# A two-layer decoder trunk on one core: first weights over two queues, joint roots for two projections

## The chip, the cores and the metric

The kernel runs on one core of a Trainium2 chip. A core has five engines that work through their own instruction queues and wait for each other by semaphores: TensorE (PE, matrix products, with its weight loads shown apart as PEld), VectorE (DVE), ScalarE (ACT), GpSimd (POOL) and SyncE (SP), which here does nothing but issue transfers. Transfers from the chip's memory run on 16 DMA engines and can be issued from several engines' queues. The metric is the time of one execution on the device in microseconds (us), smaller is better; the kernel before takes 554.64 us, the median of three runs.

## The reference

The reference is a decoder trunk of two layers over 256 tokens of width 1024, in float32. Layer 0 uses multi-head latent attention, layer 1 a block attention that, at this length, is plain causal attention with a relative bias. Both are followed by a squared-ReLU MLP.

```python
h = rms_norm(x, attn_norm[0])
proj = h @ w_in                                   # 1024 -> 384 (c_q) + 256 (c_kv) + 64 (k_pe)
q  = rms_norm(c_q, q_a_norm) @ w_uq               # 8 heads of 128 + 64
kv = rms_norm(c_kv, kv_a_norm) @ w_ukv            # 8 heads of 128 + 128
q_nope, q_pe = rms_norm(q[..., :128]), rope(rms_norm(q[..., 128:]))
k_nope, v, k_pe = rms_norm(kv[..., :128]), kv[..., 128:], rope(rms_norm(k_pe))
x = x + mla_attention(q_nope, q_pe, k_nope, k_pe, v) @ w_o
x = x + relu(rms_norm(x) @ w_in_mlp) ** 2 @ w_out_mlp
# layer 1: the same frame with moba_mixer in place of mla_mixer
```

The change touches the first product `proj`, the norms of the keys and queries of the first four heads (`k0`, `q0`), and the loading of the tables of the relative bias.

## The kernel before

**Precision and tiling.** Every large product is made of three: a float32 factor is split into a high part, rounded to the fast float32 format, and a low part, the rest, and high*high, high*low and low*high are added up in PSUM. For each piece of weights (a *unit*, up to 128 x 1024) ScalarE casts the high part (`hi`, line 176) and VectorE subtracts it for the low part (`lo`, line 185). Units are numbered in the order of use: 0 to 7 hold the rows of `w_in`, each with the matching 256 columns of the transposed input, then come nine units of the up-projections (`w_u`), the output projection and so on. `load_one` (line 151) issues the transfer of a unit on SP's queue, `load_raw` keeps a few ahead.

**Order.** The schedule is written out by hand: each engine runs its instructions in the order in which the program emits them. A call in the program is thus a place in the queue of each engine that it uses.

**First product (lines 437 to 530).** For each of the eight row blocks `make_h` (line 271) multiplies the input by the norm's gain on ScalarE (`hTh`, line 274) and makes the low part on VectorE (`hTl`, line 275). Unit 0 is cast in two column groups, the 320 key and value columns by VectorE (line 443) and the 384 query columns by ScalarE (line 445). `lat_mm` (line 459) multiplies. For unit 0 it takes the key columns of both token halves before the query columns, for the others both column groups of one token half after the other. Unit 0 also carries 42 columns of gains. The position table `rowp` is issued after unit 3 (line 233). After the sixth row block the key latent is finished, copied by ScalarE (line 515) and VectorE (line 517) and transposed by TensorE (line 505). Before that copy, ScalarE squares the token-wise input (line 472) and casts the first unit of `w_u`.

**Second stage (lines 800 to 890).** `proj0(name, t)` multiplies one projection for one token half `t`. The names are `k0`, `p` (the rotary part of the queries), `q0`, `v0`, and later `k1`, `v1`, `q1`. `post0` squares it on ScalarE, sums the squares per head (`Norm`, lines 327 to 337; with `on_act` ScalarE does the sums) and calls `root_by` (line 350): an addition of the scaled EPS on VectorE (line 353) and a power of -1/2 on GpSimd (`rsqrt_into`, line 264). `rows0` (`rows_by`, line 356) multiplies by the root on VectorE (line 358), `turn0` transposes on TensorE (line 366) and copies on ScalarE. There is one root for each name and token half. `mean_squares` (line 816) makes for each of the three latents the mean square (line 817) and its product with EPS (line 818). Beside this GpSimd turns the rotary key: two scalings (line 839), a product (line 840), two sums (line 851), and VectorE does it for the queries (`rope_rows`, lines 791 and 792; `rope_sum`, line 798). In the queue of GpSimd the scalings and the product stand ahead of the roots of `p`, the sums ahead of the roots of `q0`.

**Tables.** `table_loads` (line 253) loads the positions, spread to all partitions, and a table of key positions and bias steps in two transfers, in the first MLP.

## Time and profile before

| what | us |
|---|---|
| time, median of three runs (554.51 to 554.75) | 554.64 |
| time of the profiled execution | 554.76 |
| its span, from first to last instruction | 552.8 |
| TensorE busy | 547.9 |
| VectorE busy | 393.3 |
| ScalarE busy | 304.4 |
| GpSimd busy | 93.9 |

The span is what the trace covers; the rest of the profiled execution's time lies around it. Shares of busy time are taken over the whole span. A stage with a limit of its own, such as the first 45 us here, is read from the timeline, where each row has its start, its length, the engine, the line of the program, the operation, what it writes and reads, and in brackets how long the engine stood idle before it and for whom.

### The profile page before, as it was taken

How to read it: one execution, taken by the hardware profiler on the slowest of the kernel's cores; microseconds unless marked ns; L12 is line 12 of the kernel's file. 1: busy time of each engine (PE TensorE's matmuls, PEld its weight loads, DVE VectorE, ACT ScalarE, POOL GpSimd, SP SyncE). 2: the span in 40 equal slices, each digit the busy share in tenths (PEclk: the TensorE clock that was granted, in tenths of full speed). 3: DMA queues.
4: the chain of work that ended last, by engine and by line, in shares of the span. 5: the costliest groups of instructions: out<-in, count | busy, mean ns of one | idle time of the engine just before them, and what ended most of it. 6: DMA issues, size and time to landing. Idle time of an engine off the chain costs nothing.

```text
span 552.8 us, 11397 instructions
## 1 busy us (share of the span) xinstructions
PE 547.9 (99%) x4649; PEld 538.0 (97%) x4649; DVE 393.3 (71%) x651; ACT 304.4 (55%) x497; POOL 93.9 (17%) x109
## 2 busy tenths in 40 slices
PE   8999999999999999999999999999999999999997
PEld 7988999999999999999999999999999999999997
DVE  6897877688997689866677366766867653977630
ACT  7998675665433365445365466746755332656420
POOL 6882100031222000012232100000130311000100
PEclk9999999999999999999999999999999999999999
DMA  8854535686566466555565454345865764665810
GB/s 340 294 173 131 174 112 159 190 277 189 192 197 194 125 217 200 181 171 172 160 221 176 168 154 152 115 153 154 253 218 176 240 194 139 194 213 166 277 39 28
DMA packets 28035, 100.64 MB, mean 182 GB/s; under 512 B 3184, under 2 KB 3696, under 8 KB 27856
## 3 DMA queue, kind: packets, MB, share of 16 engines
q1 hardware_dynamic: 27648, 99.01, 55.6%
q0 software_dynamic: 336, 0.92, 0.4%
q8 instruction: 36, 0.59, 0.4%
q14 instruction: 15, 0.12, 0.1%
HBM read 98.87 MB, written 1.05 MB: 181 GB/s over the span
## 4 chain that ended last, share of the span: by engine, by line
PE 98%; DMA 1%; ACT 0%; DVE 0%; issue 0%
PE ps L85 96%; PE ps L366 2%; PE ps L588 1%; DMA xw<-in_xw 1%; PE ps L505 0%; ACT hTh L274 0%; DVE t L1062 0%; PE ps L878 0%
## 5 line engine op out<-in xcount | busy, mean ns | idle before, releaser
L185 DVE TENSOR_TENSOR wl<-raw,wh 128x1024 fp32r<-128x1024 f32 x177 | 218.5, 1252 | 35.9 <-ACT wh L176 35.3
L176 ACT CAST wh<-raw 128x1024 fp32r<-128x1024 f32 x177 | 182.7, 1047 | 69.5 <-PE ps L85 52.2
L85 PE MATMUL ps<-a,wh 128*128 128x256 f32 x1024 | 175.0, 276 | 0.0
L85 PEld LDWEIGHTS ps<-a,wh 128*128 128x128 f32 x1024 | 154.8, 188 | 0.0
L85 PE MATMUL ps<-hTl,wh 128*128 128x256 f32 x512 | 141.7, 277 | 0.0
L85 PE MATMUL ps<-a,wl 128*128 128x256 f32 x512 | 141.7, 277 | 0.0
L85 PE MATMUL ps<-hTh,wl 128*128 128x256 f32 x512 | 141.4, 276 | 0.0
L85 PE MATMUL ps<-hTh,wh 128*128 128x256 f32 x512 | 141.3, 276 | 0.0
L85 PEld LDWEIGHTS ps<-hTl,wh 128*128 128x128 f32 x512 | 96.1, 188 | 0.1
L85 PEld LDWEIGHTS ps<-hTh,wh 128*128 128x128 f32 x512 | 96.1, 188 | 0.1
L85 PEld LDWEIGHTS ps<-a,wl 128*128 128x128 f32 x512 | 96.1, 188 | 0.0
L85 PEld LDWEIGHTS ps<-hTh,wl 128*128 128x128 f32 x512 | 96.1, 188 | 0.0
L929 ACT ACTIVATE t<-ps 128x512 f32<-128x512 f32 (+1 forms) x34 | 19.4, 572 | 62.4 <-PE ps L85 62.3
L85 PE MATMUL ps<-aT,wh 128*128 128x256 f32 (+1 forms) x256 | 50.2, 288 | 0.0
L931 DVE SCALAR_TENSOR_TENSOR t<-ps,t 128x512 f32<-128x512 f32 (+1 forms) x34 | 22.4, 659 | 36.1 <-ACT t L929 35.9
L85 PE MATMUL ps<-wh,hTh 128*128 128x256 f32 (+2 forms) x224 | 45.5, 289 | 0.8 <-ACT hTh L274 0.8
L85 PE MATMUL ps<-wh,hTl 128*128 128x256 f32 (+2 forms) x224 | 44.6, 283 | 0.0
L85 PE MATMUL ps<-wl,hTh 128*128 128x256 f32 (+2 forms) x224 | 44.3, 283 | 0.0
L85 PEld LDWEIGHTS ps<-aT,wh 128*128 128x128 f32 x256 | 40.3, 188 | 0.2
L85 PE MATMUL ps<-aT,wl 128*128 128x256 f32 x128 | 35.6, 278 | 0.0
L601 ACT ACTIVATE hTh<-x,gains 128x256 fp32r<-128x256 f32 x24 | 12.2, 510 | 42.2 <-POOL x L1053 25.8
L85 PEld LDWEIGHTS ps<-wh,hTh 128*128 128x128 f32 x224 | 34.3, 188 | 1.1 <-ACT hTh L274 1.0
(167 smaller groups left out, 645.5 us busy)
## 6 DMA issues: line engine op xcount, KB each, us to landing
raw<-in_w_in_mlp SPq DMA_DIRECT2D x64, 512.0 KB, 4.3
raw<-in_w_out_mlp SPq DMA_DIRECT2D x64, 512.0 KB, 4.3
raw<-in_w_qkv SPq DMA_DIRECT2D x24, 512.0 KB, 4.4
raw<-in_w_u SPq DMA_DIRECT2D x8, 512.0 KB, 6.7
xw<-in_xw SPq DMA_DIRECT2D x7, 480.0 KB, 6.3
raw<-in_w_o0a SPq DMA_DIRECT2D x4, 512.0 KB, 3.5
raw<-in_w_o0b SPq DMA_DIRECT2D x4, 512.0 KB, 3.6
raw<-in_w_o1a SPq DMA_DIRECT2D x4, 512.0 KB, 4.2
```

The lines of the kernel that those rows point to most:

```text
L85: nc.tensor.matmul(o, a, b, start=start, stop=stop)
L176: (eng.copy if eng is nc.scalar else eng.tensor_copy)(his[i][:, :w], raws[i][:, :w])
L185: eng.tensor_sub(los[i][:, :w], raws[i][:, :w], f32(his[i][:, :w]))
L366: nc.tensor.transpose(pt[:, i * P:(i + 1) * P], yf[:, i * P:(i + 1) * P], ident)
L588: nc.tensor.transpose(pt[:, i * P:(i + 1) * P], self.p[:, i * P:(i + 1) * P], ident)
L601: nc.scalar.activation(hTh[:, k], x[:, k], AF.Copy, scale=gain(gname, k))
L929: nc.scalar.activation(rl, src, AF.Relu)
L931: nc.vector.scalar_tensor_tensor(sq, src, 0.0, rl, op0=OP.max, op1=OP.mult)
```

## The change

- Unit 0 comes in two transfers on SP's queue: first the 320 key and value columns with the input and the gains, then the 384 query columns. Weights now stand ahead of the input in a unit. Unit 1 is issued on ScalarE's queue instead of SP's, and `rowp` follows after unit 1 instead of unit 3.
- For row block 0 ScalarE makes `hTh` for the first 128 tokens and VectorE for the others. Unit 1 is cast in the two column groups, and its products take the key columns of both token halves first, like those of unit 0.
- `k0` and `q0` have one root for both token halves: the sums of squares go side by side into one tile, and after the second half one VectorE instruction adds EPS and one GpSimd power makes both roots. `p`, `k1` and `q1` keep a root for each half.
- The product with EPS of the rotary key's mean square, which nothing reads, is left out.
- In the second stage the projection and the root of `p`'s first half are emitted ahead of the rotary key's scalings and product; `k0`'s second rows go behind the `hi` and `lo` that followed them; `q0`'s second half goes ahead of the `lo` and of `p`'s second rows. `hi` keeps its place among ScalarE's instructions.
- The rings of the small norm tiles have 16 divided by their width buffers instead of 4.
- The positions stand in the table, and one transfer loads both.

```diff
@@ -153,9 +153,10 @@
             raw = early.tile([P, S + n + (0 if i else NG)], F32, name=f"xw{i}")
-            nc.sync.dma_start(raw, src)
-            x0.append(raw[:, :S])
-            raws.append(raw[:, S:S + n])
+            for c in (slice(QR, S + n + NG), slice(0, QR)) if i == 0 else (slice(0, S + n),):
+                (nc.scalar if i == 1 else nc.sync).dma_start(raw[:, c], src[:, c])
+            raws.append(raw[:, :n])
+            x0.append(raw[:, n:S + n])
             if i == 0:
@@ -229,14 +230,14 @@
         load_one()
-        if k == 3:
+        if k == 1:
             nc.sync.dma_start(rowp, A["rowp"])
...
     load_raw()
-    pos_row = const.tile([P, S], I32)
-    tables = const.tile([P, S // 4 + 8 * H], I32)
-    pos_k4, tcur, tprev = (tables[:, :S // 4], *(f32(tables[:, S // 4 + i * 4 * H:S // 4 + (i + 1) * 4 * H]) for i in range(2)))
+    tables = const.tile([P, S + S // 4 + 8 * H], I32)
+    pos_row, pos_k4 = tables[:, :S], tables[:, S:S + S // 4]
+    tcur, tprev = (f32(tables[:, S + S // 4 + i * 4 * H:S + S // 4 + (i + 1) * 4 * H]) for i in range(2))
     ident = const.tile([P, P], F32)
@@ -251,7 +252,6 @@
     def table_loads():
-        nc.sync.dma_start(pos_row, A["pos_row"].to_broadcast([P, S]))
         nc.sync.dma_start(tables, A["tables"])
@@ -271,7 +271,10 @@
         g = gain(gname, k) if k else gains0[0][:, GOFF[gname][0]:GOFF[gname][0] + 1]
-        nc.scalar.activation(hTh[:, k], x0[k], AF.Copy, scale=g)
+        n = S if k else P
+        nc.scalar.activation(hTh[:, k, :n], x0[k][:, :n], AF.Copy, scale=g)
+        if n < S:
+            nc.vector.tensor_scalar(hTh[:, k, n:], x0[k][:, n:], g, None, op0=OP.mult)
         nc.vector.scalar_tensor_tensor(hTl[:, k], x0[k], g, f32(hTh[:, k]), op0=OP.mult, op1=OP.subtract)
@@ -324,10 +327,10 @@
-        def __init__(self, p, width, on_act=False):
+        def __init__(self, p, width, on_act=False, ss=None):
             self.p, self.width, self.nh = p, width, 512 // width
             j = t2(512)
-            self.ss = small.tile([P, self.nh], F32, name="hss", tag=f"hss{self.nh}")
+            self.ss = small.tile([P, self.nh], F32, name="hss", tag=f"hss{self.nh}", bufs=16 // self.nh) if ss is None else ss
             if on_act:
@@ -337,7 +340,7 @@
         def root(self, sq):
-            self.rs = small.tile([P, self.nh], F32, name="hrs", tag=f"hrs{self.nh}")
+            self.rs = small.tile([P, self.nh], F32, name="hrs", tag=f"hrs{self.nh}", bufs=16 // self.nh)
             nc.vector.tensor_scalar(self.ss, self.ss, sq, EPS, op0=OP.mult, op1=OP.add)
@@ -349,7 +352,7 @@
-            self.rs = small.tile([P, self.nh], F32, name="hrs", tag=f"hrs{self.nh}")
+            self.rs = small.tile([P, self.nh], F32, name="hrs", tag=f"hrs{self.nh}", bufs=16 // self.nh)
             nc.vector.tensor_scalar(self.ss, self.ss, 1.0 / self.width, e, op0=OP.mult, op1=OP.add)
@@ -437,7 +440,13 @@
     for k in range(KD):
-        if k == 0:
+        if k == 1:
+            his.append(wsp.tile([P, 1024], F32R, name="wh", tag="wh"))
+            make_h(k, "attn0")
+            for c in win_parts:
+                nc.scalar.copy(his[1][:, c], raws[1][:, c])
+            lo()
+        elif k == 0:
             his.append(wsp.tile([P, 1024], F32R, name="wh", tag="wh"))
@@ -472,7 +481,7 @@
     for k in range(KD - 2):
-        if k == 0:
+        if k < 2:
             for i in range(3):
@@ -764,17 +773,29 @@
-    def post0(name, t, root=True, on_act=False):
+    pairs = {}
+
+    def post0(name, t, on_act=False):
         p = open_p.pop((name, t))
...
             nc.scalar.activation(flat(hd[int(name[1])]["v"][:, t]), p, AF.Copy, scale=scl[:, 0, t:t + 1])
-        else:
-            norms[name, t] = Norm(p, PE_D if name == "p" else P, on_act)
-            if root:
-                root0(name, t)
-
-    def root0(name, t):
-        norms[name, t].root_by(epsm[:, 0 if name[0] == "k" else 2, t:t + 1])
+            return
+        width = PE_D if name == "p" else P
+        if name in ("p", "k1", "q1"):
+            norms[name, t] = Norm(p, width, on_act)
+            norms[name, t].root_by(epsm[:, 0 if name[0] == "k" else 1, t:t + 1])
+            return
+        if t == 0:
+            pairs[name] = small.tile([P, NT, 512 // width], F32, name="pss_" + name, bufs=1)
+        norms[name, t] = Norm(p, width, on_act, pairs[name][:, t])
+        if t == NT - 1:
+            ss, n = pairs[name], 512 // width
+            rs = small.tile([P, NT, n], F32, name="prs_" + name, bufs=1)
+            e = epsm[:, 0 if name[0] == "k" else 1, :, None].to_broadcast([P, NT, n])
+            nc.vector.scalar_tensor_tensor(ss, ss, 1.0 / width, e, op0=OP.mult, op1=OP.add)
+            rsqrt_into(rs, ss)
+            for i in range(NT):
+                norms[name, i].rs = rs[:, i]
@@ -811,15 +832,16 @@
     msl = small.tile([P, 3, NT], F32, name="msl", bufs=1)
-    epsm = small.tile([P, 3, NT], F32, name="epsm", bufs=1)
-
-    def mean_squares(i, n):
+    epsm = small.tile([P, 2, NT], F32, name="epsm", bufs=1)
+
+    def mean_squares(i, n, j=None):
         nc.vector.scalar_tensor_tensor(msl[:, i], ssl[:, 1 + i], 1.0 / n, me0, op0=OP.mult, op1=OP.add)
-        nc.vector.tensor_scalar(epsm[:, i], msl[:, i], EPS, None, op0=OP.mult)
+        if j is not None:
+            nc.vector.tensor_scalar(epsm[:, j], msl[:, i], EPS, None, op0=OP.mult)
     nc.vector.tensor_scalar(me0, ssl[:, 0], EPS / D, EPS * EPS, op0=OP.mult, op1=OP.add)
-    mean_squares(0, KVR)
     mean_squares(1, PE_D)
+    mean_squares(0, KVR, 0)
     scl = small.tile([P, 2, NT], F32, name="scl", bufs=1)
@@ -830,22 +852,22 @@
     heads_ctx, hd, aT = head_tiles(0)
-    mean_squares(2, QR)
+    mean_squares(2, QR, 1)
...
     ks = t2(NT, PE_D)
+    proj0("p", 0)
+    post0("p", 0)
     for t in range(NT):
...
     nc.gpsimd.tensor_mul(m, ks[:, :, None, :].to_broadcast([P, NT, 2, PE_D]), ropek)
-    proj0("p", 0)
-    post0("p", 0)
     rows0("k0", 0)
...
     post0("p", 1)
-    rows0("k0", 1)
     hi()
     lo()
+    rows0("k0", 1)
     for o, a, b in rope_halves(m[:, :, 0], m[:, :, 1]):
@@ -854,10 +876,10 @@
     hi()
+    proj0("q0", 1)
+    post0("q0", 1, on_act=True)
     lo()
     rows0("p", 1)
-    proj0("q0", 1)
-    post0("q0", 1, on_act=True)
     rope_sum(0)
@@ -1207,8 +1229,8 @@
-    xw = np.concatenate([lay(np.asarray(x)[0].T, (KD, P, S), (0, 1, 2)),
-                         lay(np.asarray(mla_w_in)[0], (KD, P, 704), (0, 1, 2))], axis=2)
+    xw = np.concatenate([lay(np.asarray(mla_w_in)[0], (KD, P, 704), (0, 1, 2)),
+                         lay(np.asarray(x)[0].T, (KD, P, S), (0, 1, 2))], axis=2)
@@ -1225,8 +1247,7 @@
         "rowp": rowp,
-        "pos_row": np.ascontiguousarray(pos[None]),
-        "tables": np.concatenate([np.repeat(lay(pos, (S // 4, 4), (1, 0)), 32, axis=0)]
+        "tables": np.concatenate([np.tile(pos[None], (P, 1)), np.repeat(lay(pos, (S // 4, 4), (1, 0)), 32, axis=0)]
                                  + [t.reshape(P, 4 * H).view(np.int32) for t in (tcur, tprev)], axis=1),
```

## The prediction

> **What bounds the kernel now.** I read the page first, then the chain that ended last in order of time, then the timeline of the first 45 us engine by engine, because nearly all edits act there.
>
> ```profile
> PE 547.9 (99%) x4649; PEld 538.0 (97%) x4649; DVE 393.3 (71%) x651; ACT 304.4 (55%) x497; POOL 93.9 (17%) x109
> PE 98%; DMA 1%; ACT 0%; DVE 0%; issue 0%
> 0.73 3.72 DMA xw<-in_xw
> 4.47 0.52 ACT hTh L274
> ```
>
> TensorE is busy 99% of 552.8 us, and the chain that ended last is 98% TensorE. What is not TensorE is the front: 3.72 us until the first unit has landed and 0.52 us for its first scaled half. So an edit is worth only what it makes TensorE start earlier or stand still less. The profiled execution took 554.76 us (span 552.8, 1.96 around it), 0.12 over the median of 554.64; I add my sum to the median.
>
> **The front.** Bytes first:
>
> ```profile
> 2.00:3.00 1.00, 1.00 (x4) 0.45 (x3) 0.00 (x0) 0.20 (x1) 0.97 (x4) 1.00 0.60 212
> 3.00:4.00 1.00, 1.00 (x7) 0.37 (x4) 0.00 (x0) 0.00 (x0) 0.00 (x0) 1.00 1.00 387
> 6.00:12.00 6.00, 6.00 (x40) 6.00 (x39) 5.50 (x10) 5.67 (x11) 3.47 (x4) 1.00 1.03 414
> 12.00:18.00 6.00, 6.00 (x40) 6.00 (x39) 5.08 (x13) 5.56 (x10) 5.24 (x10) 1.00 1.03 409
> xw<-in_xw SPq DMA_DIRECT2D x1, 501.0 KB, 3.7
> xw<-in_xw SPq DMA_DIRECT2D x7, 480.0 KB, 6.3
> ```
>
> The last number is GB/s: 212, then 387, then a flat 410 up to 18 us. The transfers form one full stream; after the opening only their order can change. And what TensorE meets at 18.5 us hangs on that stream:
>
> ```profile
> 4.88 0.49 ACT L445 CAST wh<-xw 128x384 fp32r<-128x384 f32 x1
> 5.03 1.02 PE L85 MATMUL ps<-wh,hTh 128*128 128x320 f32 x4 [0.82 <-ACT hTh L274]
> 5.72 0.51 ACT L274 ACTIVATE hTh<-xw,gains 128x256 fp32r<-128x256 f32 x1 [0.34 <-DMA xw<-in_xw]
> 17.02 1.05 ACT L176 CAST wh<-raw 128x1024 fp32r<-128x1024 f32 x1 [0.21 <-DMA raw<-in_w_u]
> 17.97 0.42 ACT L515 COPY ckv<-ps 128x320 f32<-128x320 f32 x1
> 18.54 0.41 PE L505 MATMUL ps<-ident,ckv 128*128 128x128 f32 x2
> ```
>
> ScalarE's cast at 17.02 waits for the ninth unit to land, its copy of the key latent comes behind it and ends at 18.39, and TensorE's transposes at 18.54 read that copy. If TensorE is early, it waits there: the slack is 18.54 less 18.39 less about 0.06 for the signal, 0.09 us. The number of bytes up to that landing is unchanged, so **an earlier first matmul gains about nothing, while a later one costs all but 0.09**.
>
> Now the sides. The first half transfer is 618 of 1002 columns, 309 KB. Alone it saves 192 KB / 410 GB/s, some 0.5 us, and the half-width ScalarE pass saves about 0.2: the first matmul at about 4.3 instead of 5.03. But only two matmuls use these columns before the next two want the query columns, which come in the second half and then need the 0.49 us cast. TensorE's first unit therefore shifts as that cast does: landing of the second half, against 4.88 now. Without company it lands near 4.45 (-0.4). If the second unit goes beside it, 501 and 480 KB share the stream and the last of them lands when both now have, 5.7 (ScalarE's row at 5.72): +0.8. A fuller opening of the stream (212 against 410 GB/s between 2 and 3 us) can give at most 0.5 of that back. Which it is depends on when ScalarE issues:
>
> ```profile
> 0.72 1.28 ACT L225 ACT_TABLE_LOAD   x1 [0.72 <-PEq L1240]
> 2.01 0.20 ACT L225 ACTIVATE warm<-warm 128x1 f32<-128x1 f32 x1
> 28.86 0.60 ACT L336 ACTIVATE t<-ps 128x512 f32<-128x512 f32 x1 [0.44 <-PE ps L85]
> L334 ACTq EVENT_SEMAPHORE  x4: 17/17/1548, 28.9 to 42.4; - x4
> ```
>
> The new issue stands behind the table load and the warm-up activation. At 28.9 the sequencer already handles a wait of L334 while L336 still runs and a cast stands between, so it runs ahead, and I take an issue near 0.9 us, beside unit one. Sum: +0.8, less 0.09, less half of what the opening may give (0.25): **+0.4**, ends -0.1 and +0.7. An issue only at 2.2 would share just the second half: about +0.1. The position table moves ahead of unit three, 81 KB or 0.2 us; units three and on have that to spare (480 KB are 1.2 us of stream, and a unit's 12 matmuls 1.8: 40 of them fill the 6 us of the window from 6 to 12).
>
> [...]
>
> **The middle.** From 29.3 to 42.9 us VectorE never rests, and TensorE waits for it:
>
> ```profile
> 36.00:42.00 6.00, 5.92 (x33) 4.27 (x32) 6.00 (x14) 5.76 (x18) 3.57 (x4) 1.00 0.65 246
> 33.79 0.30 PEld L85 LDWEIGHTS ps<-wl,ckvT 128*128 128x128 f32 x2 [0.42 <-DVE wl L185]
> 37.19 0.30 PEld L85 LDWEIGHTS ps<-wl,ckvT 128*128 128x128 f32 x2 [0.33 <-DVE wl L185]
> 38.65 0.97 PEld L366 LDWEIGHTS ps<-ident,t 128*128 128x128 f32 x8 [0.29 <-issue]
> 28.01 0.23 DVE L353 TENSOR_SCALAR hss<-hss,epsm 128x4 f32<-128x4 f32 x1
> 29.47 0.17 DVE L818 TENSOR_SCALAR epsm<-msl 128x2 f32<-128x2 f32 x1
> 30.26 0.30 DVE L353 TENSOR_SCALAR hss<-hss,epsm 128x8 f32<-128x8 f32 x1
> 32.52 1.21 DVE L185 TENSOR_TENSOR wl<-raw,wh 128x1024 fp32r<-128x1024 f32 x1
> 35.92 1.21 DVE L185 TENSOR_TENSOR wl<-raw,wh 128x1024 fp32r<-128x1024 f32 x1
> 37.79 0.75 DVE L798 TENSOR_TENSOR t<-t,t 128x256 f32<-128x256 f32 x2
> 38.46 0.69 DVE L358 TENSOR_TENSOR t<-ps,hrs 128x512 f32<-128x512 f32 x1
> ```
>
> *Removed from VectorE:* one product with EPS (0.17), and one of two root additions each for k0 and q0 (0.23): some 0.5 us by 38 us. *Moved:* the low split of the value unit (32.52) goes ahead of k0's second rows (0.68), so it starts near 31.7 and the 0.42 wait at 33.79 goes; the split at 35.92 comes to 35.5 and the 0.33 wait goes. The pipeline hides part of such waits; I count 0.25 and 0.15. The rope sum ends near 38.0 instead of 38.54, so the 0.29 at 38.65 goes too. Up to the transposes of q0's first half TensorE would be 0.45 early. What is late next is **q0's root on GpSimd**:
>
> ```profile
> 30.23 0.87 POOL L839 TENSOR_SCALAR t<-ckv,scl 128x64 f32<-128x64 f32 x2
> 31.19 0.74 POOL L840 TENSOR_TENSOR t<-t,ropek 128x256 f32<-128x256 f32 x1
> 31.89 1.66 POOL L264 TENSOR_TENSOR hrs<-hss,mhalf 128x8 f32<-128x8 f32 x1
> 35.20 2.25 POOL L851 TENSOR_TENSOR t<-t 128x128 f32<-128x128 f32 x2
> 37.41 2.00 POOL L264 TENSOR_TENSOR hrs<-hss,mhalf 128x4 f32<-128x4 f32 x2
> 41.67 1.22 DVE L185 TENSOR_TENSOR wl<-raw,wh 128x1024 fp32r<-128x1024 f32 x1
> 41.84 1.91 POOL L264 TENSOR_TENSOR hrs<-hss,mhalf 128x4 f32<-128x4 f32 x1 [2.43 <-DVE hss L353]
> ```
>
> A root costs by its columns: 1.00 for 4 (two in 2.00), 1.66 for 8. So a joint root saves 0.34 in sum, but its first half is ready 0.66 later. And a GpSimd operation that starts under a low split stands until the split ends: the one at 41.84 began under the split of 41.67 to 42.89 and ended 0.86 after it, as the second sum of 35.20 ended 0.32 after the split at 35.92. Walk GpSimd's new order: p's first root 30.4 to 32.05 (its addition ends at 30.56 today and 0.15 earlier then; it now precedes the two scalings, whose 0.87 had been done by 31.1); the scalings fall under the moved split (31.7 to 32.95) and end at 33.7; the product 0.74, 34.4; p's second root 1.66, with a short hold by VectorE's rope products, 36.2; the two sums, some 0.45 each without their holds (2.25 less 0.5 under a rope product and 0.9 under the split), the first held by the split until 36.7, 37.5; q0's joint root 1.66, **39.1**. Today q0's first root is done at 38.43, and VectorE takes it up at 38.46. So q0's first rows start 0.65 later, VectorE waits 1.1 us at the head of its queue, and behind it stand q0's second rows, p's second rope rows and sum, which TensorE's next transposes and the first logits need; the 0.45 won before is waited off. **+0.65.** The bounds: with no hold at all the list ends at 30.4 + 1.66 + 0.87 + 0.74 + 1.66 + 0.9 + 1.66 = 37.9, before VectorE comes at 38.0: then -0.45. With another full hold of 0.75: +1.4.
>
> [...]
>
> **At nothing:** the loss of one position load at about 95 us and the larger table (TensorE has no wait there; uncovered, one 128 KB transfer of 5.0 us); the layout of a unit; the smaller rings of 4 and 2 buffers; the two-part cast of the second unit, 0.15 us more on ScalarE, under 1.9 us of matmuls.
>
> Sum: +0.4 + 0.65 = +1.05; 554.64 + 1.05 = **555.7**.
>
> **Rivals.**
> - *GpSimd is on time* (no or little hold): -0.45 in the middle with -0.1 to +0.4 in front: 554.1 to 554.6. For: without the holds it is; against: two of its operations start under the moved splits.
> - *Late issue by ScalarE*: front +0.1, middle +0.65: 555.4. Against: the row at 28.9.
> - *Slower still:* k0's joint root is caught too.
>
> ```profile
> 26.89 1.04 ACT L176 CAST wh<-raw 128x1024 fp32r<-128x1024 f32 x1
> 28.15 1.22 DVE L185 TENSOR_TENSOR wl<-raw,wh 128x1024 fp32r<-128x1024 f32 x1
> ```
>
>   Its addition (28.01 to 28.24 today, less 0.17 and one addition) ends about 27.8; the split behind it can start when ScalarE's cast is done, 27.93. If the split is first, the root waits until 29.17 and ends at 30.6 instead of 29.5; past 30.3 VectorE stands. Price 0.35, with the front at its +0.7: 554.64 + 0.7 + 0.65 + 0.35 = 556.3. It decides at 0.1 us.
> [...]
> - *Faster:* two queues fill the opening (up to -0.5 on the whole stream, and so at 18.5), GpSimd is on time, and the small waits of 39 to 44 us shrink too: -1.2, 553.4.
>
> **How the numbers follow.** Forecast 0.45 (555.1 to 556.1), on time 0.20, late issue 0.10, slower still 0.13, lock 0.02, faster 0.10. About 0.2%, 1.1 us, is what a measurement of this kernel can tell from no change. The forecast lies just inside it: of its 0.45 I give 0.18 to slower. Slower 0.18 + 0.13 + 0.02 = 0.33, same 0.27 + 0.20 + 0.10 = 0.57, faster 0.10. Range 553.9 to 556.4: it takes in the on-time case with its lower end and the slower one, and leaves out the faster case and the lock.
>
> **What the profile after would show.** Front: the issue on ScalarE's queue near 0.9 (or 2.2); the cast of the query columns at 5.3 to 5.7 with a TensorE wait before the third matmul; the transposes of L505 later than 18.54. Middle: no weight-load waits for the splits near 34 and 37; q0's root of 8 columns ending near 39.1; VectorE idle about 1 us before q0's first rows, released by GpSimd. Wrong if the query columns are cast before 4.9, if L505 comes before 18.4, or if q0's root ends before 38.4.

## The result and the profile after

The changed kernel takes **558.06 us** in the median of six executions (556.95 to 558.85), beside 554.62 (554.50 to 554.76) for the kernel before on the same chip: a ratio of 1.0058, with a 95% interval of 1.0047 to 1.0068. It is slower, and outside the range that was forecast. The six times lie in two groups, 556.95 to 557.48 and 558.64 to 558.85; the profiled execution is one of the longer ones (558.85, span 556.7).

The page after, its busy times:

```profile
PE 550.2 (99%) x4649; PEld 540.2 (97%) x4649; DVE 392.5 (70%) x649; ACT 304.6 (55%) x498; POOL 91.2 (16%) x107
q10 hardware_dynamic: 144, 0.49, 0.2%
```

VectorE and GpSimd have less to do than before, as the diff says, and a second load queue is there: unit 1 alone, 128 packets of a row each and 16 of 4 bytes. TensorE's 4649 products are the same in number. The time is again lost where TensorE starts or stands. The chain that ended last, in order of time (start, length, what):

```profile
1.17 4.96 DMA xw<-in_xw
6.15 0.52 ACT wh L454
6.72 14.76 PE ps L85 x82
...
37.21 2.07 POOL hrs L264
39.28 1.03 POOL t L873 x2
40.31 1.80 POOL prs_q L264
42.13 0.69 DVE t L361
```

Before, this chain left the first landing at 4.45 us by way of the scaled input of row block 0. Now it comes from the **second transfer of unit 0**, issued at 1.17 and landed at 6.13, by the cast of the query columns; and later it runs through GpSimd's queue to q0's joint root. These are the two places that the prediction named.

How far TensorE is behind the kernel before, instruction by instruction, from the two traces (start before, start after, difference):

```
first product of unit 0 (key columns)     5.03    4.92   -0.11
third product (query columns)             5.43    6.72   +1.28
first product with hTl                    5.89    7.52   +1.63
first product with wl                     6.53    8.69   +2.16
first product of unit 1                   7.17    9.87   +2.70
transposes of the key latent             18.54   21.32   +2.78
transposes of p's first half             38.69   40.99   +2.30
transposes of q0's first half            39.21   42.97   +3.76
end of the last instruction             552.83  556.73   +3.90
```

TensorE in the kernel after (in brackets the idle time before, and for whom):

```profile
4.92 0.88 PE L85 MATMUL ps<-wh,hTh 128*128 128x320 f32 x2 [0.27 <-ACT hTh L275]
6.72 1.01 PE L85 MATMUL ps<-wh,hTh 128*128 128x384 f32 x2 [0.91 <-ACT wh L454]
7.52 1.38 PE L85 MATMUL ps<-wh,hTl 128*128 128x320 f32 x4
8.69 1.38 PE L85 MATMUL ps<-wl,hTh 128*128 128x320 f32 x4
9.87 0.88 PE L85 MATMUL ps<-wh,hTh 128*128 128x320 f32 x4
10.58 0.81 PE L85 MATMUL ps<-wh,hTl 128*128 128x320 f32 x4
```

and, for comparison, the same products before:

```profile
5.89 0.80 PE L85 MATMUL ps<-wh,hTl 128*128 128x320 f32 x4
6.53 0.80 PE L85 MATMUL ps<-wl,hTh 128*128 128x320 f32 x4
```

Two things happen in the front. TensorE stands 0.91 us for the cast of the query columns. And behind that stand each group of four products takes 1.38 us instead of 0.80, until about 10 us: it runs at **half its clock**. The trace's first record of a granted clock is a full one at 10.01 us, against 3.605 in the kernel before. For the time ahead of its first record a trace tells nothing of the clock (the views print 1.00 there), so the half is read from the products: in e7 below, groups of four that take 1.36 and 1.38 us lie in a stretch with a recorded clock of 0.50. The slow products add 1.5 us (from +1.28 to +2.78), more than the stand itself.

ScalarE after; its second row waits for the landing of the query columns:

```profile
4.45 0.40 ACT L275 ACTIVATE hTh<-xw 128x128 fp32r<-128x128 f32 x1 [2.23 <-DMA xw<-in_xw]
6.15 0.51 ACT L454 CAST wh<-xw 128x384 fp32r<-128x384 f32 x1 [1.30 <-DMA xw<-in_xw]
```

The first transfer lands at 4.42, hardly before the whole unit of the kernel before (4.45), and the query columns at 6.13. This execution is a late one in both: in seven other profiled executions with the same front (e2, e4, e5, e7, e8, e12, e13) they land at 3.93 to 4.16 and at 5.58 to 5.84. Over the opening of the stream (last column GB/s) the kernel after has

```profile
2.50:3.50 1.00, 1.00 (x4) 0.38 (x3) 0.00 (x0) 0.00 (x0) 0.48 (x2) 1.00 0.68 247
```

where the kernel before has

```profile
2.50:3.50 1.00, 1.00 (x4) 0.38 (x3) 0.00 (x0) 0.00 (x0) 0.47 (x2) 1.00 0.98 357
```

so in these profiles two queues opened the stream more slowly, not faster. The seven others with this front have 279 to 349 GB/s in that stretch, the six other profiled executions with one queue 339 to 382. Why is not shown; e16, which has two queues as well, has 366.

The middle, GpSimd and then VectorE after:

```profile
33.13 1.64 POOL L264 TENSOR_TENSOR hrs<-hss,mhalf 128x8 f32<-128x8 f32 x1 [0.95 <-DVE hss L356]
34.76 1.62 POOL L863 TENSOR_SCALAR t<-ckv,scl 128x64 f32<-128x64 f32 x2
36.46 0.75 POOL L864 TENSOR_TENSOR t<-t,ropek 128x256 f32<-128x256 f32 x1
37.15 2.13 POOL L264 TENSOR_TENSOR hrs<-hss,mhalf 128x8 f32<-128x8 f32 x1
39.26 1.05 POOL L873 TENSOR_TENSOR t<-t 128x128 f32<-128x128 f32 x2
40.28 1.82 POOL L264 TENSOR_TENSOR prs_q<-pss_q,mhalf 128x8 f32<-128x8 f32 x1
```

```profile
38.29 0.15 DVE L795 SCALAR_TENSOR_TENSOR pss_q<-pss_q,epsm 128x8 f32<-128x8 f32 x1
38.37 1.21 DVE L186 TENSOR_TENSOR wl<-raw,wh 128x1024 fp32r<-128x1024 f32 x1
42.13 0.69 DVE L361 TENSOR_TENSOR t<-ps,prs_q 128x512 f32<-128x512 f32 x1 [1.20 <-POOL prs_q L264]
```

The waits for the moved splits are gone (the shift goes from +2.78 to +2.30). GpSimd then works with hardly a gap from 33.1 to 42.1; q0's sums of squares are ready at 38.44, but its root starts only at 40.28, and VectorE stands 1.20 us for it: +1.46 at q0's transposes.

### The profile page after: what moved, and what is told of

Read it like the earlier page. It is cut to its first block, busy times and chain, and to the rows that moved or that the text cites. A ratio compares the mean times of both kernels' runs of the same rounds, so it can differ in the third digit from the quotient of the medians.

```text
span 556.7 us, 11391 instructions
## 1 busy us (share of the span) xinstructions
PE 550.2 (99%) x4649; PEld 540.2 (97%) x4649; DVE 392.5 (70%) x649; ACT 304.6 (55%) x498; POOL 91.2 (16%) x107
## 3 DMA queue, kind: packets, MB, share of 16 engines
HBM read 98.87 MB, written 1.05 MB: 179 GB/s over the span
## 4 chain that ended last, share of the span: by engine, by line
PE 94%; POOL 2%; ACT 1%; DVE 1%; DMA 1%; issue 0%; SPq 0%
PE ps L85 92%; PE ps L369 1%; PE ps L597 1%; DMA xw<-in_xw 1%; POOL hrs L264 1%; ACT xs L481 0%; ACT wh L177 0%; POOL prs_q L264 0%; POOL t L863 0%; DVE wl L186 0%; ACT cqT L518 0%; POOL t L873 0%; ACT t L339 0%; DVE t L361 0%; DVE t L819 0%
```

## The experiments

Theory: the front costs by late query columns and by a late clock; the middle by q0's joint root at the end of GpSimd's queue. Rivals: the front is harmless and all of the loss lies in the middle; the joint root is late by itself, wherever it is queued; the position rows, moved ahead, slow the stream down. Differences below are to the median of the kernel before on the same chip: 554.84 for e1 to e4, 554.92 for e5 to e8, 554.78 for e9 to e12, 554.72 for e13 to e15, 554.89 for e16.

### First four: the queue, the joint root, the clock

**e1**, unit 1 on SyncE's queue:

```diff
-                (nc.scalar if i == 1 else nc.sync).dma_start(raw[:, c], src[:, c])
+                nc.sync.dma_start(raw[:, c], src[:, c])
```

> The changed kernel, but unit 1 is issued on SP's queue again; unit 0 keeps its two transfers. Theory (the second unit beside the first delays the query columns, TensorE stands 1.3 us and then runs 1.4 us of work at half clock): the query columns land near 4.6 instead of 6.1, their cast is at about 4.7 instead of 6.15, the first unit's products are over near 7.0 instead of 9.87, no stretch at half clock, and the middle keeps its +1.1: 555.4 to 556.0. Rival (two transfers for unit 0 are the cost, through smaller rows): the query cast stays after 5.5 and the time above 557.

557.49 us (557.16 to 557.81), +2.65. The query columns were cast early, as expected, and yet little was won:

```profile
3.61 0.40 ACT L275 ACTIVATE hTh<-xw 128x128 fp32r<-128x128 f32 x1 [1.39 <-DMA xw<-in_xw]
4.09 0.51 ACT L454 CAST wh<-xw 128x384 fp32r<-128x384 f32 x1
6.90 0.51 ACT L275 ACTIVATE hTh<-xw,gains 128x256 fp32r<-128x256 f32 x1 [2.30 <-DMA xw<-in_xw]
```

Now it is unit 1 that lands late, at 6.81 instead of 5.63. The suspicion was the position rows, which go ahead of unit 2; e9 and e14 test it.

**e2**, own roots for the first queries, and **e3**, the edits of e1 and e2 together:

```diff
-        if name in ("p", "k1", "q1"):
+        if name in ("p", "q0", "k1", "q1"):
```

> The changed kernel, but q0 has a root for each token half again; everything else stays. Theory (the joint root on GpSimd ends 1.2 us after VectorE wants it): q0's first root ends 0.7 earlier on GpSimd, VectorE's wait before q0's first rows shrinks from 1.2 to about 0.5, the time falls by 0.6 to 0.8 to about 557.3. Rival (the moved splits and the new order of GpSimd are the cost, not the joint root): the wait stays near 1.2 and the time within 0.3 of 558.1.

> Both edits of the two runs before: unit 1 on SP's queue and own roots for q0. If front and middle are separate causes, the gains add: 558.1 - 2.4 - 0.7 = 555.0. If the middle only shows while the front is late, the gain is that of the front alone.

575.82 us (574.33 to 575.93) and 574.56 (574.45 to 574.73): 20 us longer, and nothing in the first 45 us explains it. The window of 100 us in the middle of e2:

```profile
100.00:200.00 100.00, 100.00 (x861) 99.86 (x861) 75.54 (x115) 46.49 (x59) 18.01 (x15) 1.00 0.60 187
```

and of the kernel after:

```profile
100.00:200.00 100.00, 100.00 (x901) 99.88 (x900) 80.39 (x121) 50.01 (x63) 17.84 (x15) 1.00 0.60 193
```

TensorE is busy all the time in both, at full clock, and gets through 861 products in place of 901. The edit drops 64 bytes a partition from the pool of small tiles, so that all tiles behind it lie elsewhere; products of 256 columns start 0.119 us apart in the mean instead of 0.114. Both runs say nothing on the roots; e8 repeats e2 with the addresses kept.

**e4**, five constant products that keep TensorE at work between the two column groups of unit 0; they write a PSUM tile that nobody reads:

```diff
                     for t in range(NT):
                         lat_mm(lat[t], g, t, k, i)
+                    if (k, i, g) == (0, 0, 1):
+                        pz = ps()
+                        for _ in range(5):
+                            mm(pz[:, :S], one.to_broadcast([P, P]), one.to_broadcast([P, S]), True, True)
```

> The changed kernel with five products of constants (256 columns) on TensorE between the first two products of unit 0 and the next, where TensorE waits for the query columns; their result is not read. Clock theory (the half speed from 7.2 to 9.9 us comes because TensorE stood before): the first products of units 0 and 1 run at full speed (0.15 us for 320 columns instead of 0.27), all runs fall near the faster ones of the changed kernel, 557.0 to 557.3, and the 558.6 to 558.9 group is gone. Rival (the half speed does not come from the standing, or the five products only delay): 558 or more, with the half-speed stretch still there.

556.93 us (556.87 to 557.15, five executions), +2.09. The longer group is gone. TensorE in e4:

```profile
4.99 0.73 PE L85 MATMUL ps<-const-bfloat16-1.0 128*128 128x256 bf16 x5
6.39 0.62 PE L85 MATMUL ps<-wh,hTh 128*128 128x384 f32 x2 [0.67 <-ACT wh L454]
6.85 0.80 PE L85 MATMUL ps<-wh,hTl 128*128 128x320 f32 x4
```

The products run at full speed right behind the wait. In this execution the full clock was there from 4.53, ahead of the five products; that they help is read from the times, not from this trace. What stays is the wait for the query columns: TensorE is 0.96 behind at 6.39.

### The two halves of the change by themselves

**e6**, the change without its front (unit 0 in one transfer, unit 1 on SyncE's queue, position rows behind unit 3, casts and `make_h` as before):

```diff
-            for c in (slice(QR, S + n + NG), slice(0, QR)) if i == 0 else (slice(0, S + n),):
-                (nc.scalar if i == 1 else nc.sync).dma_start(raw[:, c], src[:, c])
+            nc.sync.dma_start(raw, src)
...
-        if k == 1:
+        if k == 3:
             nc.sync.dma_start(rowp, A["rowp"])
...
```

> The kernel after with the whole front of the kernel before: unit 0 in one transfer, unit 1 whole and on SyncE's queue, the position rows behind unit 3, scaling and casts of k = 0 and 1 as before; joint roots, moved splits and the merged tables stay. Theory (the front costs 1.0 to 2.7, the middle 1.1): full clock granted at about 3.6, the products before 28 us at the times of the kernel before to 0.1, then -0.4 at 37 and +1.45 at the turns of q0: 555.5 to 556.2. Rival (the front is harmless in most executions, the middle costs the difference): 556.9 or more.

555.88 us (555.63 to 556.41, ten executions), **+0.96**: the price of the middle, as the theory said. In its trace TensorE is 0.42 early at the transposes of `p` (38.27 for 38.69) and 1.04 late at those of q0 (40.25 for 39.21). GpSimd's joint root and VectorE's row that waits for it, in e6:

```profile
37.55 1.83 POOL L263 TENSOR_TENSOR prs_q<-pss_q,mhalf 128x8 f32<-128x8 f32 x1
39.41 0.69 DVE L357 TENSOR_TENSOR t<-ps,prs_q 128x512 f32<-128x512 f32 x1 [1.20 <-POOL prs_q L263]
```

**e7**, the front alone, in the kernel before: the hunks on `load_one` with the new order of a unit's columns, `rowp`, `make_h`, the casts of unit 1 and the order of its products, and nothing else.

```diff
-            nc.sync.dma_start(raw, src)
+            for c in (slice(QR, S + n + NG), slice(0, QR)) if i == 0 else (slice(0, S + n),):
+                (nc.scalar if i == 1 else nc.sync).dma_start(raw[:, c], src[:, c])
...
-        if k == 3:
+        if k == 1:
             nc.sync.dma_start(rowp, A["rowp"])
...
```

> The kernel before with the front of the change alone: unit 0 in two transfers, unit 1 on ScalarE's queue, position rows behind unit 1, query columns of both units by themselves; own roots, the order of the splits and the tables as before. Theory (the query columns of unit 0 land behind unit 1, which costs about 1.0, and TensorE's full clock comes late in many executions, which adds up to 1.5): 555.6 to 557.4, and the clock granted between 4.5 and 10 us. Rival (the front costs nothing once the stream of transfers is full, as it sets the end of the first stage): 554.5 to 555.0.

557.11 us (556.86 to 558.54), +2.2. The profiled execution is the one at 558.54, and shows the clock as no other does. Windows of it (the stretch, its length, busy time and count of PE, PEld, DVE, ACT and POOL, the granted clock, DMA share, GB/s):

```profile
3.38:6.79 3.41, 1.71 (x10) 1.06 (x9) 1.88 (x5) 1.41 (x4) 2.02 (x5) 1.00 1.02 391
6.80:10.20 3.40, 3.40 (x13) 3.40 (x13) 3.00 (x6) 3.00 (x6) 3.14 (x5) 0.50 1.03 415
10.21:13.60 3.39, 3.39 (x22) 3.39 (x22) 3.36 (x8) 3.30 (x7) 3.07 (x4) 1.00 1.02 413
```

The full clock had come at 3.38. In the 3.41 us that follow, TensorE is busy for 1.71 only, as it waits for the query columns; then the clock is halved for 3.41 us, in which 13 products run where the next window holds 22. The three records, 3.382, 6.796 and 10.209, lie 3.414 and 3.413 us apart. So here 3.41 us in which TensorE was busy for half of the time were followed by 3.41 us at half clock. By what rule the clock is set is not shown. The first record of a full clock comes at other times in other executions (3.38 here, 4.53 in e4, 4.77 in e8, 10.01 in the kernel after); that the times differ with it is my reading of the groups of executions.

The three shorter executions of e7 stand at +1.9 to +2.2, not at +1.0. Its trace shows one more loss: TensorE is 2.46 behind the kernel before when its slow products are over, and 3.19 behind from 38 us on, after a stand of 0.30 for VectorE's split at 36.97. The moved splits of the kernel after take these waits away. So the prices of the front and of the middle are not two fixed amounts that add up. Another 0.74 of this execution arises behind its last product and is not explained.

### q0's root

**e5**, the scalings and the product of the rotary keys ahead of `p`'s first root again, and **e13**, the same once more:

```diff
-    proj0("p", 0)
-    post0("p", 0)
     for t in range(NT):
         nc.gpsimd.tensor_scalar(ks[:, t], ckv[:, t, KVR:], scl[:, 1, t:t + 1], None, op0=OP.mult)
     nc.gpsimd.tensor_mul(m, ks[:, :, None, :].to_broadcast([P, NT, 2, PE_D]), ropek)
+    proj0("p", 0)
+    post0("p", 0)
```

> The kernel after, with one edit: the three GpSimd instructions that scale and turn the rotary keys (L863 twice, L864) stand again ahead of proj0('p', 0) and so ahead of the two roots of p on GpSimd's queue, as in the kernel before; the joint roots stay. Theory (the joint root of the first queries is late because it is queued behind the rotary work, which moved behind p's first root and there met a split of VectorE): p's first root starts some 0.7 later, the second ends near 37.0 instead of 39.3, the key sums near 38.1, q0's joint root near 40.2 instead of 42.1, VectorE's wait of 1.20 ahead of L361 goes down to about 0.2, and the time falls by 1.0 to 1.3: 555.9 to 556.5 where the clock comes as in the shorter executions of the kernel after, 557.5 where it comes late. Rival (a joint root is late by itself, because both halves wait for the second one's squares): the first rows of q0 stay at 41.8 or later, gain under 0.4.

> e5 once more, unchanged. Theory (the executions at 557.4 have a late clock): if this profile is of one near 557.4, the full clock comes between 6.4 and 10 us in it and the products of units 0 and 1 run at half speed until then, while the middle is as in e5; if it is near 555.9, the clock comes before 6.2. Rival (two ways of falling in the middle): a profile near 557.4 with an early clock, and another order of GpSimd's and VectorE's work between 30 and 42 us.

e5: 555.89 in the profiled execution, 557.38 to 557.62 in three others. e13: 555.97 in the median, five executions at 555.70 to 556.09 and three at 557.23 to 557.33. GpSimd and VectorE in e5:

```profile
30.40 0.88 POOL L861 TENSOR_SCALAR t<-ckv,scl 128x64 f32<-128x64 f32 x2
32.06 3.30 POOL L264 TENSOR_TENSOR hrs<-hss,mhalf 128x8 f32<-128x8 f32 x2
37.08 2.56 POOL L264 TENSOR_TENSOR prs_q<-pss_q,mhalf 128x8 f32<-128x8 f32 x1
```

```profile
36.92 1.21 DVE L186 TENSOR_TENSOR wl<-raw,wh 128x1024 fp32r<-128x1024 f32 x1
39.68 0.69 DVE L361 TENSOR_TENSOR t<-ps,prs_q 128x512 f32<-128x512 f32 x1 [0.27 <-POOL prs_q L264]
```

The two scalings take 0.88 instead of 1.62, GpSimd's queue is empty for the joint root at 37.08, and VectorE's wait falls from 1.20 to 0.27, though the root is now held by a split that starts ahead of it (2.56 instead of 1.64). Between the two kernels with the five constant products (e12 below, +1.09, and e4, +2.09) the edit is worth 1.00, between the two with the front of before (e10 below, +0.51, and e6, +0.96) 0.45. The queue ahead of the root was half of its price or more. Both profiles of this kernel are of the shorter group, so that the longer one has a late clock is not seen directly.

**e12**, e5 with the five constant products of e4:

> e5 with the five constant products of e4 that keep TensorE at work while the query columns are awaited. Theory (e5's executions at 557.4 are late clocks): all executions at 555.7 to 556.3, the wait of 1.0 for the query columns staying as the front's price. Rival (they come from the middle): some executions at 557.2 to 557.6 again.

555.87 us, nine of ten executions from 555.52 to 556.01, one at 556.83. The executions at 557.3 are gone with the stand bridged, which speaks for the clock; the one at 556.83 stays unexplained.

**e8**, e2 with the addresses kept:

```diff
     pairs = {}
+    for i in range(2):
+        small.tile([P, NT, 4], F32, name=f"room{i}", bufs=1)
...
-        if name in ("p", "k1", "q1"):
+        if name in ("p", "q0", "k1", "q1"):
```

> As e2 (own roots for the first queries in the kernel after), with two unused tiles of 32 bytes a partition in the small pool, so that all later tiles keep their addresses. Theory (e2's 20 us came from the shifted addresses; the joint root itself is worth 0.6): 256-column products at a pitch of 0.1135 again, time 556.3 to 556.7 with an early clock and 558.1 with a late one, VectorE's wait ahead of q0's first rows 0.58 instead of 1.20. Rival (e2's loss came from the own roots in some way): 574 to 576 again.

556.38 us, seven executions at 556.15 to 556.47 and two at 557.75. The 20 us of e2 are gone, so they were the addresses. Own roots are worth 0.63 against e4, VectorE waits 0.58 instead of 1.20. TensorE in it, an execution whose clock came early (4.77 us) with the same late query columns:

```profile
6.43 0.62 PE L85 MATMUL ps<-wh,hTh 128*128 128x384 f32 x2 [1.19 <-ACT wh L454]
6.88 0.80 PE L85 MATMUL ps<-wh,hTl 128*128 128x320 f32 x4
```

Here the front costs the stand alone: 6.43 for 5.43, +1.00.

**e10**, e6 with the edit of e5, and **e11**, e10 with own roots for q0 as in e8:

> e6 (the front of before) with the rotary keys' scaling ahead of p's roots again, as in e5; joint roots stay. Theory: q0's joint root ends 0.9 to 1.0 earlier against the stream than in e6, the middle costs +0.1 to +0.3 in all, and nothing depends on the clock: 554.9 to 555.3 in all executions. Rival (e5's three executions at 557.4 beside the profiled one at 555.9 come from the middle, in two ways of falling, and not from a late clock): some executions at 555.0, others at 556.5.

> e10 with own roots for the first queries, the pool's size kept. Of the change there remain the moved splits, k0's joint root, the merged tables and the new order of the unit's columns. Theory (the moved splits are worth 0.4, and the price of q0's joint root is all that stood against them): 554.4 to 554.8 beside before's 554.6 to 554.9, so 0.0 to 0.4 faster. Rival (VectorE, which is busy from 30 to 38 without a gap, only hands the split's delay on to q0's first rows): 554.9 to 555.3, no gain.

555.29 us (555.05 to 555.68), +0.51, and 555.01 (554.78 to 555.78), +0.23, a ratio of 1.0004 with an interval of 0.9995 to 1.0013. So what stays of the change when both losses are taken out is no gain that can be measured. In e11's trace TensorE is 0.27 early at 38.41 and 0.12 at the end: q0's rows start at 38.28 on a VectorE that has no gap, and hardly sooner than before (38.46). What the moved splits win waits there.

### Why the query columns come late

**e9**, e1 with the position rows behind unit 3 again, and **e14**, the kernel after with that alone (`if k == 3` for `if k == 1`):

> e1 (unit 1 on SyncE's queue, unit 0 in two transfers) with the position rows behind unit 3 again, as before. Theory (in e1 the 648-byte rows of the position table, moved ahead of unit 2, mixed into unit 1's packets and made it late; an early first unit gains nothing, as the stage is set by the stream of transfers): unit 0's halves land by 3.6 and 4.1, unit 1 by about 5.3 instead of 6.8, unit 2 near 6.5, TensorE doesn't stand between the two column groups, the transposes of L514 stand where L505's stood before (18.5 to 18.7), and the end is that of e6: 555.6 to 556.2. Rival A (the early start carries through to the end): 554.6 to 555.2. Rival B (the position rows have nothing to do with it): unit 1 at 6.8 again, 557.2 to 557.8.

> The kernel after with the position rows behind unit 3 again; split and second queue stay. Theory (the 81 KB of position rows share the stream ahead of the end of the query columns, 0.2 us at 410 GB/s, the rest of the delay is the shared stream itself): query columns land at 5.9 to 6.0, a gain of 0.1 to 0.2: 556.8 to 557.3 with an early clock. Rival (small rows slow the whole stream down): 5.6 or earlier, gain 0.4 or more.

e9: 557.61 us (557.50 to 557.83), +2.83, and unit 1 lands later still:

```profile
4.06 0.51 ACT L454 CAST wh<-xw 128x384 fp32r<-128x384 f32 x1
7.32 0.51 ACT L275 ACTIVATE hTh<-xw,gains 128x256 fp32r<-128x256 f32 x1 [2.75 <-DMA xw<-in_xw]
```

e14: 558.37 us (556.69 to 558.51), and the query columns land at 5.96. The suspicion against the position rows has fallen: with the rows out of the way the query columns land no earlier than in the seven other executions with the rows ahead (5.58 to 5.84). A cost of 0.2 us, what 81 KB take at 410 GB/s, can't be read from single executions that differ by more. In e9 unit 1's share is done by 4.88 to 5.21 on nine of the sixteen DMA engines, and only by 6.10 to 7.23 on the other seven. Why those stand with a transfer outstanding, on one queue behind two short ones, remains open.

**e15**, the second queue without the split of unit 0:

```diff
-            for c in (slice(QR, S + n + NG), slice(0, QR)) if i == 0 else (slice(0, S + n),):
+            for c in (slice(0, S + n + (0 if i else NG)),):
```

> The kernel after with unit 0 in one transfer on SyncE's queue, unit 1 on ScalarE's queue as in the change. Theory (two queues share the engines' time about equally, so the first unit is late by about half of what the second takes): unit 0 lands at 5.3 to 5.7 instead of 4.45, the first product comes near 5.9 instead of 5.03, TensorE stands 1.7 us from 4.13 on, units 2 on as in before; 556.4 to 557.2 with an early clock, and late clocks more often than in the kernel after. Rival (the second queue adds throughput and the first unit keeps its time): unit 0 by 4.8, 555.8 to 556.2 as e6.

555.96 us (555.79 to 556.27, ten executions), +1.24: e6's time to 0.3, and no longer group. ScalarE in e15:

```profile
4.80 0.40 ACT L275 ACTIVATE hTh<-xw 128x128 fp32r<-128x128 f32 x1 [2.58 <-DMA xw<-in_xw]
5.11 0.50 ACT L454 CAST wh<-xw 128x384 fp32r<-128x384 f32 x1
```

Unit 0 lands at 4.77 and unit 1 at 5.67. They don't share the stream half and half: unit 1's 480 KB are 1.2 us of stream at 410 GB/s, and 0.90 of these lie behind unit 0's landing. The rival had the landing and the time right; that a second queue adds throughput is not shown. So the second queue alone is nearly harmless. Late query columns take both, the split and the second queue; the split alone (e1, e9) costs as much in another way, by a late unit 1.

**e16**, the two swapped: the query columns on ScalarE's queue, unit 1 on SyncE's:

```diff
-                (nc.scalar if i == 1 else nc.sync).dma_start(raw[:, c], src[:, c])
+                (nc.scalar if (i, c.start) == (0, 0) else nc.sync).dma_start(raw[:, c], src[:, c])
```

> The kernel after with the two contending transfers swapped: the query columns of unit 0 on ScalarE's queue (issue near 0.89), unit 1 on SyncE's (issue near 1.17). Theory (transfers are served in the order of their issue over both queues): first half of unit 0 by about 4.1, query columns by 4.6 instead of 6.13, unit 1 by about 5.8, no stand of TensorE between the column groups; the front costs nothing, the middle stays: 555.6 to 556.2 in all executions, as e6 and e15. Rival (a transfer behind a half unit on SyncE's queue is starved, as unit 1 was in e1 and e9): unit 1 at 6.8 or later, 557.2 to 557.8.

556.62 us (556.22 to 557.28, ten executions), +1.73. The landings came as expected, 3.68, 4.18 and 5.41; the time did not. TensorE starts at 4.40 and stands nowhere until 8.83, and still:

```profile
18.22 0.45 PE L85 MATMUL ps<-wl,hTh 128*128 128x320 f32 x2
19.03 0.41 PE L514 MATMUL ps<-ident,ckv 128*128 128x128 f32 x2 [0.35 <-ACT ckv L524]
```

It waits for ScalarE's copy of the key latent and is 0.49 later than before at these transposes. An early front is not carried to the end of the stage, because the stream of transfers sets that end: the eighth unit, the last of the first product, lands at 13.56 in e16 and at 13.09 in the kernel before. Between 4.5 and 6.0 us the stream of e16 moved only 252 to 329 GB/s; why remains open.

In the kernel after the order of landing is first part of unit 0, unit 1, query columns (4.42, 5.62, 6.13); in e16 it is first part, query columns, unit 1 (3.68, 4.18, 5.41); in e15 unit 0, unit 1 (4.77, 5.67). Each is the order in which the transfers were issued over both queues (in the kernel after 0.73 SyncE, 0.89 ScalarE, 1.17 SyncE). By what rule the DMA engines choose between two queues is not shown.

## Why the prediction failed, step by step

The forecast was +1.05, and the range ended at 556.4, which is +1.76. With an early clock the change costs +2.09 (e4), so the time would have lain beyond the range even without the loss by the clock. Two terms of the sum were too small, the front's and the middle's, and one was missing: the half-speed products behind TensorE's stand, 1.5 us in the profiled execution.

- **ScalarE issues near 0.9.** Right: the trace has the issue at 0.894, while the table load runs (0.72 to 2.00).
- **An earlier first product gains nothing.** Right, and for the reason given, the stream: e6 starts 0.39 early, at 4.64, its eighth unit lands at 13.09 as before, and its transposes of the key latent come at 18.55 where the kernel before has them at 18.54. e16 starts 0.63 early, lands 0.47 later and is 0.49 late there. e11 starts 0.21 early, lands 0.21 earlier (12.88) and is 0.19 early (18.34).
- **The query columns land at 5.7, which costs +0.8 gross and +0.4 net.** The mechanism and the landing were right, the net price was too small. They landed at 5.58 to 5.84 in seven profiled executions and at 6.13 in the kernel after, and the stand put TensorE 1.00 behind in e8 and 0.96 in e4. The 0.25 that was taken off for a fuller opening had the wrong sign: 247 GB/s between 2.5 and 3.5 us where the kernel before has 357, and 279 to 349 in the seven others. (0.8 less 0.09 less 0.25 is also 0.46, put down as 0.4.)
- **A later first matmul "costs all but 0.09".** This is the step that failed. The delay itself came through as forecast: 1.00 at e8's third product is 0.99 at its transposes of the key latent. But the price of a late start was taken to be that delay alone, and the clock stood at nothing in the sum. In e7 a stretch of 3.41 us in which TensorE was busy for 1.71 was followed by one at half clock, and in the kernel after the products behind the stand of 0.91 us ran at half speed. These products cost 1.5 us in the profiled execution, and by my reading make the longer group: 15 of 35 executions of the kernels that have the late query columns (after, e5, e7, e8, e13, e14) are longer by 1.4 us or more than the shortest of the same kernel. The three profiled executions of longer groups (after, e7, e14) have half speed right behind the stand, until 10.01, 10.21 and 9.44, the three of shorter groups (e5, e8, e13) have the full clock from 4.32, 4.77 and 5.73 on. With the stand bridged or taken away (e4, e6, e10, e11, e12, e15, e16) it is none of 67. Of 91 executions of the kernel before on the same chips one is longer by as much (557.04); its cause is not known.
- **The moved splits win 0.45.** Right: 0.42 in e6.
- **q0's joint root ends at 39.1, and VectorE waits 1.1 us.** Right in its mechanism, the GpSimd walk too. In e6, whose front is that of before, the root ended at 39.38 and VectorE waited 1.20. The size of the result was short: +0.65 was forecast, from a root that ends at 39.1; e6 has +1.04 at q0's transposes and +0.96 in the time. Two GpSimd roots were held under VectorE's work for longer than I allowed: `p`'s second took 2.13 and q0's 1.83, for 1.66 each.
- **Rivals.** No run shows the lock that the chances give 0.02, a split of VectorE held by a GpSimd root that started ahead of it: e6's root of k0 runs from 27.81 for 1.64, and the split that starts under it at 27.97 takes 1.23, beside a mean of 1.25 over the 177 splits of the kernel after. k0's root was not caught by the split either. "Slower still" had the right sign and the wrong mechanism.

The sum by the runs, in the kernel after: front +1.0, middle +1.0, which is e4's +2.09; with a late clock 1.5 more. In the kernel before the front alone costs more (e7, +1.9 to +2.2). The three shorter executions of the kernel after stand at +2.3 to +2.9, so some 0.2 to 0.8 of these isn't assigned to anything; e4 and the kernel after were not measured side by side.

## What to carry to other kernels

A wait of TensorE in the first microseconds is to be priced twice: as time (0.91 us in the kernel after), and as a clock that came several us later there (10.01 for 3.605) or went away again (e7, from 6.80 to 10.20). Half a transfer landed hardly sooner here than the whole (4.42 for 4.45), and its second half, overtaken by unit 1 (5.62), at 6.13: look at which transfers are issued between the two halves, on every queue. And a joint operation on an engine that works in order is worth its saved start only if its queue is empty when the *last* of its inputs comes; here 0.34 us of GpSimd time was to be saved, and 1.0 was lost, because the first half had to wait for the second and both for the rotary keys.

## What the runs showed of the hardware

- The records of the granted clock in e7 are 3.414 and 3.413 us apart, and a stretch in which TensorE was busy for 1.71 of 3.41 us was followed by one at half clock. The busy share alone doesn't set the two apart in these runs: in the kernel before a stretch of that length busy for 0.83 (0.19 to 3.60) was followed by the full clock, in e14 one busy for 0.86 (2.62 to 6.03) by half speed until 9.44.
- 64 bytes a partition less in an early pool made the same products slower at full clock: 861 for 901 in 100 us (e2), and 20 us on the whole kernel. With the bytes put back they were gone (e8). Whoever compares two versions of such a kernel has to keep the addresses of the later tiles.
- With two short transfers ahead of it on one queue, unit 1 landed at 6.81 (e1) and 7.23 (e9) instead of 5.63, held up by 6 and 7 of the 16 DMA engines; with the second of the two on another queue it landed at 5.41 (e16), and the stream fell off behind it instead.
